# Constant matmuls while the first input is awaited, spread memsets, own weight tiles for the third and fourth product, and systems in four transfers

## The chip, the cores and the metric

The kernel runs on one core of a Trainium2 chip. A core has engines that work side by side, each on its own queue of instructions, in order: TensorE (PE in the profile; PEld is its weight load), VectorE (DVE), ScalarE (ACT), GpSimd (POOL) and SyncE (SP, which here issues all transfers). They wait for each other on semaphores. The metric is the device time of one execution in microseconds (us); lower is better.

## What is computed

One layer of a streaming encoder for a prompt of 2048 frames and 32 sample frames, 1024 wide. The input is normalised and projected once (about 6160 columns); branch A is attention over a band of nine 64-frame chunks, branch B a gated delta rule in chunks of 64; both are gated, merged, projected and normalised again.

```
hp = layer_norm(x_prompt, ln0_g, ln0_b)
qa, ka, va, za, qkv_b, zb, a_b, b_b, gate_a, gate_b = split_projection(x @ w_in)
...
ya = (oa.reshape(bsz, t, A_WIDTH) * jax.nn.silu(za)) @ w_branch_a
...
t_inv = lax.linalg.triangular_solve(eye + m, jnp.broadcast_to(eye, m.shape),
                                    left_side=True, lower=True, unit_diagonal=True)
...
yb = (ob * jax.nn.silu(zb)) @ w_branch_b
mix = jax.nn.sigmoid(gate_a) * ya + jax.nn.sigmoid(gate_b) * yb
y = layer_norm(ALPHA * x + mix @ w_out, ln_g, ln_b)
```

## The kernel before

**Who sets the order.** The program's text does not give the order of the instructions. Each piece of work is a Python generator (a stream) that yields where it must wait: for a gate (a number of buffers), a mark (something is done), a queue, or a time. `Flow.run` takes the stream whose own clock is least, lets it emit instructions up to its next yield, and advances clocks by a price of each instruction (`Engine.price`, lines 225 to 254) and of each transfer (`Flow.transfer`, 203 to 209: 200 KB per us behind the transfers planned before it). So prices decide in which order instructions stand in each engine's queue. On the chip the engines then work through these queues in order, each instruction waiting for its operands. All engine instructions but a few are emitted at line 260, all transfers at line 283; a tile's name therefore tells more than a line.

**The opening.** `build_h(0, ...)` brings the first 1024 frames in as eight tiles `x` of 128 frames. For each: mean and variance on DVE (`BATCH_NORM_STATS2`, `BATCH_NORM_AGGREGATE` into `mv`), a power on POOL, the scaling of `x` on DVE, eight transposes on PE into two PSUM banks (`b` and `a`), scale and shift into `tmp` (the first half by ACT, the second by DVE), the high float16 half `hi` (cast on ACT) and the rest `lo` (POOL). `norm_params` first brings the scale and shift vectors `ln0gT` and `ln0bT` by a transpose of `prm`, and derives their common scale `h_scale` by a small product.

**The projection.** Each column group of 128 of `w_in` is a `Job`. `fetch` loads its weights (`wraw`, two buffers); `divide` finds a power-of-two scale from the sum of squares (ACT `Square` into `whi`, a product `b<-w_sq,tiny` on PE, `w_scale` on DVE, POOL, DVE), scales on ACT, casts to `whi` (ACT) and subtracts into `wlo` (POOL). There are two pairs of `whi` and `wlo`, and `divide` asks for one at `w_gate` before anything else. `multiply` then makes 8 products `whi` x `hi`, 8 `wlo` x `hi` and 8 `whi` x `lo` for each block of columns, into a bank `pj`. The first two jobs are gates of the merge; their blocks, 256, 256 and 512 columns wide, alternate (`two`), so that both use each part of the input as it comes. The third job is `ab` (16 columns: decay and beta of the delta rule, with `whi` alone), the fourth the first of the convolution's. When the last block of a job is multiplied, its pair goes back to `w_gate`. `marked` is the generator that hands the jobs out, two late, so that the last two of a half can be marked.

**Branch B.** When the input of a half is there, `phase_b` opens. `diag` makes 17 tiles that hold block diagonals (`k_bd`, `qk_bd` four each, `q_bd`, `kd_bd`, `u_bd` three each), and clears each with a memset on DVE, one behind the other. Eight blocks of 512 frames (and the sample, in the second half) go through `prep` (decays), `system` (the triangular systems, written to DRAM as `sol_p` in four transfers), `solve` (brings them back so that each of 128 partitions holds one of 32 systems, four times over for four groups of right-hand sides, in `sys_p`; then 31 steps of two DVE instructions on `sys_t` and `sys_u`), `inverse`, and `chain` (the recurrence over chunks, PE and DVE by turns: banks `x`, tiles `r`, `vn`, `state`). Two `solve` streams run side by side. The transfer into `sys_p` has an access pattern whose slowest dimension has four steps of no distance: `[[0, 4], [1024, 32], [1, 1024]]`.

**Then** branch A of the half, the second half with the same two phases, and the merge with the output projection.

The names that the change touches: `Flow.transfer`, `norm_params` (a neighbour is added), `Job`, `divide`, `multiply`, `phase_b` (`diag`, `system`, `solve`, the list of streams that it starts), `marked`, and the opening and the loop at the end of `trunk`.

Of the kernel before, what the change touches and what calls it, by code (L numbers as in the profile page):

```python
# [21 lines left out]
P = 128  # L22
# [34 lines left out]
for _p in range(1, NP):  # L57
    ORDER += [(_p, 0), (_p, 1), (_p, 2), (_p - 1, 3)] + [None] * FILL[_p]
ORDER += [(NP - 1, 3)]
MARGIN = 1.6  # L60
LEAD = 5.0
BLOCKS = [
    [(0, 512, 0), (512, 512, 512)],
# [91 lines left out]
class Flow:  # L155
# [47 lines left out]
    def transfer(self, queue, size):  # L203

        start = max(self.cur.clock + 0.2, self.busy.get(queue, 0.0)) + 0.5
        self.busy[queue] = start
        end = max(start + 0.6, self.busy.get("DMA", 0.0)) + size / 200e3
        self.busy["DMA"] = end
        return end + MARGIN
# [59 lines left out]
def trunk(ctx: ExitStack, tc: tile.TileContext, x_p, x_s, cache_k, cache_v, st_conv, st_gdn,  # L269
# [89 lines left out]
    def power(out, sums):  # L359

        yield bank["b"]
        ps = pt("b")
        PE.matmul(ps[:, 0:1], tiny[:], sums, start=True, stop=True)
        yield
        V.tensor_scalar(out=out, in0=ps[:, 0:1], scalar1=1e-24, scalar2=None, op0=ALU.add)
        bank["b"].give()
        yield
        rsqrt(out, out)
        yield
        V.tensor_scalar(out=out.bitcast(I32), in0=out.bitcast(I32), scalar1=0x7F800000, scalar2=None,  # L370
                        op0=ALU.bitwise_and)

    def norm_params(sp):
# [197 lines left out]
    class Job:  # L571
# [3 lines left out]
        def __init__(self, half, wid, src, evac=None, key=None, cols=P, blocks=None):  # L575
            self.wid = wid
            self.half, self.src, self.evac, self.cols, self.key = half, src, evac, cols, key
            self.end = self.two = False
            self.blocks = blocks or BLOCKS[half]

# [42 lines left out]
    def divide():  # L623

        while True:
            job, raw, t = yield from q_raw.get()
            yield w_gate
            hi = wpool.tile([P, KD, P], F16, tag="whi", bufs=2, name="whi")
            lo = wpool.tile([P, KD, P], F16, tag="wlo", bufs=2, name="wlo")
            sc = w_scale[:, job.wid:job.wid + 1]  # L630
# [36 lines left out]
    def multiply():  # L667

        while True:
            some, todo = [], [(0, 0)]  # L670
            while todo:
# [26 lines left out]
                for k in range(KD):  # L698
                    PE.matmul(ps[:, 0:n], wh[:, k], hl[:, k, :], start=False, stop=(k == KD - 1))
                    if k == KD - 1:  # L700
                        last = bi == len(job.blocks) - 1
                        if job.end and (bi == 0 or last):
                            h_free[0 if bi == 0 else 1].give()
                        if last:
                            w_gate.give()
# [80 lines left out]
    def phase_b(half):  # L786
# [21 lines left out]
        def diag(name, bufs):  # L808
            ts = []
            for i in range(bufs):  # L810
                t = bp.tile([P, 8, P], F32, name=f"{name}{i}")
                V.memset(t[:], 0.0)
                ts.append(t)
            return ts

        k_bd, qk_bd = (diag(n, NPAR) for n in ("k_bd", "qk_bd"))
# [354 lines left out]
        def system(k):  # L1171
# [4 lines left out]
            yield k.qk_ready  # L1176
            yield k.prep
            k.pn = yield from p_slots.take()
            kb, qkb = k.kb, k.qkb = k_bd[k.par], qk_bd[k.par]
# [45 lines left out]
        def solve():  # L1225
            while True:
# [5 lines left out]
                for g in range(4):  # L1232
                    G.memset(sys_u[g * 32:(g + 1) * 32].rearrange("p r i -> p (r i)")[:, g::36], 1.0)
                yield t
                p0 = pd[k.n % (2 * NP)][:]
                yield dma(sys_p[:].rearrange("p j i -> p (j i)"),
                          bass.AP(p0.tensor, p0.offset, [[0, 4], [1024, 32], [1, 1024]]))
                yield from substitute(sys_p, sys_u, sys_t)
# [196 lines left out]

        for g in (worker(todo), worker(decays), prep(), local(), solve(), solve()):
            flow.start(g)
# [506 lines left out]
    def marked():  # L1944

        ahead, half = [], None
        for job in all_jobs():
            if job.half != half:
# [4 lines left out]
                job.two = True  # L1953
            n += 1
            if n <= 2:
                if job.key is None:
# [267 lines left out]


    with ExitStack() as stack0:
        open_banks(stack0, "ps0", a=3)
        xp = stack0.enter_context(tc.tile_pool(name="x0", bufs=1, reuse_waits="tile"))
        flow.start(norm_params(xp))
        flow.start(build_h(0, xp, 8))  # L2230
# [7 lines left out]
    for half in range(2):  # L2238
        stack, make, done = phase_b(half)
        enter(1, half, make)  # L2240
        flow.run(done)
        stack.close()
        if half:
            wr_pool.append(ctx.enter_context(tc.tile_pool(name="wr0", bufs=1)))
# [71 lines left out]
```

## Time and profile before

| what | value |
|---|---|
| time, median of 3 runs | 2083.18 us (2080.98 to 2087.81) |
| the profiled execution | 2081.13 us, of which the span (first to last instruction) is 2079.4 |
| PE busy / idle in the span | 1969.9 / 109.5 us |
| granted TensorE clock, mean over the span | 0.982 |
| DVE, ACT, POOL busy | 1456.5, 977.0, 709.3 us |
| transfers, all queues | 196.5 MB, 95 GB/s on average |

How to read the rows that follow: in the timeline a row has its start in us from the span's start, its length, the engine, line, operation, `out<-in`, the shape, and in brackets how long the engine had been idle before it and what ended that. Matmuls are pipelined, so the length of one is longer than the step from one to the next. In the table of windows a row has the stretch, its length, the busy time of each engine with its number of instructions, the granted clock of TensorE (PEclk), the mean busy share of 16 DMA engines and what they moved in GB/s. In the list of waits a row has who waited for whom, the sum in us, how often, and the longest.

### The profile page before, as it was taken

What the parts mean: (1) busy time and instruction counts of PE and PEld (TensorE: products, weight loads), DVE (VectorE), ACT (ScalarE), POOL (GpSimd) and SP (SyncE); (2) the same over time, 40 slices, a digit from 0 to 9 for tenths busy, and PEclk for the clock granted to TensorE, in tenths of its full rate; (3) what the DMA queues carried; (4) which work ended last, traced back from release to release, by engine and by line L of the source; (5) the groups of instructions that cost most, each with busy time, mean ns of one, the idle gap of its engine ahead of it and who ended that gap; (6) DMA issues with size and microseconds to landing.
All of it is one profiled execution on the core that took longest, in us unless ns stands there. A gap on an engine that the chain in (4) does not pass through costs nothing. (4 is left out here: it accounts for less than half of the span.)

```text
span 2079.4 us, 41810 instructions
## 1 busy us (share of the span) xinstructions
PE 1969.9 (95%) x15098; PEld 1419.4 (68%) x15098; DVE 1456.5 (70%) x4673; ACT 977.0 (47%) x2098; POOL 709.3 (34%) x1075
## 2 busy tenths in 40 slices
PE   4899999999999999899999899999999999999998
PEld 3455666667465666566677676767667678999996
DVE  7579888874267667768998887347657677655565
ACT  5565645444466668564544434346566642111110
POOL 5254443423322123334333323311110224644443
PEclk9899999999999999999999999999999999999999
DMA  3132332232323333222233233332332345433331
GB/s 109 62 98 80 98 107 65 82 82 87 121 68 122 92 87 101 66 72 73 78 85 88 73 91 95 97 91 76 87 89 82 108 139 196 135 105 113 111 123 48
DMA packets 197724, 196.53 MB, mean 95 GB/s; under 512 B 79623, under 2 KB 147571, under 8 KB 197517
## 3 DMA queue, kind: packets, MB, share of 16 engines
q1 hardware_dynamic: 197516, 193.85, 31.7%
q8 instruction: 119, 1.95, 0.4%
q14 instruction: 89, 0.72, 0.1%
HBM read 135.91 MB, written 50.53 MB: 90 GB/s over the span
## 5 line engine op out<-in xcount | busy, mean ns | idle before, releaser
L260 PE MATMUL pj<-hi,whi 128*128 128x512 f16 (+2 forms) x1992 | 654.3, 344 | 12.6 <-POOL whi L260 2.4
L260 PE MATMUL pj<-hi,wlo 128*128 128x512 f16 (+2 forms) x1952 | 644.4, 342 | 2.0 <-POOL wlo L260 1.9
L260 PEld LDWEIGHTS <-whi 128*128 128x128 f16 x3984 | 412.7, 105 | 222.2 <-issue 11.1
L260 PE MATMUL pj<-lo,whi 128*128 128x512 f16 (+2 forms) x1992 | 461.3, 339 | 0.0
L260 POOL TENSOR_TENSOR wlo<-wraw,whi 128x256 f16<-128x256 f32 x384 | 263.8, 708 | 570.9 <-ACT whi L260 328.4
L260 PEld LDWEIGHTS <-wlo 128*128 128x128 f16 x1952 | 207.1, 106 | 112.6 <-issue 11.2
L260 ACT CAST mh<-sg 128x256 fp32r<-128x256 f32 x64 | 26.0, 407 | 273.7 <-DVE sg L260 273.7
L260 ACT ACTIVATE wraw<-wraw,w_scale 128x1024 f32<-128x1024 f32 (+1 forms) x98 | 111.5, 1138 | 64.9 <-DVE w_scale L260 51.9
L260 ACT CAST ph<-b 128x512 f16<-128x512 f32 (+2 forms) x224 | 92.9, 422 | 100.2 <-PE b L260 95.4
L260 PE MATMUL a<-ghi,whi 128*128 128x256 f32 (+1 forms) x512 | 132.5, 290 | 4.9 <-DVE sg L260 4.7
L260 DVE TENSOR_TENSOR pl<-b,ph 128x512 f16<-128x512 f32 (+2 forms) x224 | 107.2, 485 | 37.9 <-ACT ph L260 36.8
L260 PE MATMUL a<-ghi,wlo 128*128 128x256 f32 (+1 forms) x512 | 130.6, 286 | 1.1 <-DVE wlo L260 1.1
L260 ACT CAST whi<-wraw 128x512 f16<-128x512 f32 (+1 forms) x196 | 119.6, 611 | 23.4 <-PE pj L260 20.5
L260 DVE TENSOR_TENSOR sys_u<-sys_u,sys_t 128x60 f32<-128x60 f32 (+24 forms) x527 | 123.3, 240 | 6.1
L260 POOL TENSOR_TENSOR w_scale<-w_scale,mhalf 128x1 f32<-128x1 f32 x49 | 32.4, 662 | 257.0 <-DVE w_scale L260 204.0
L260 ACT ACTIVATE sb<-sb,mx,unit 128x640 f32<-128x640 f32 (+4 forms) x128 | 108.8, 851 | 20.7 <-DVE mx L260 20.3
L260 DVE SCALAR_TENSOR_TENSOR acc<-raw,cwT,acc 128x512 f32<-128x512 f32 x144 | 112.0, 777 | 5.2 <-ACT acc L260 4.1
L260 DVE TENSOR_TENSOR sys_t<-sys_u,sys_p 128x60 f32<-128x60 f32 (+20 forms) x459 | 111.2, 246 | 5.9
L260 PEld LDWEIGHTS a<-ghi,whi 128*128 128x128 f32 x512 | 98.2, 192 | 7.3 <-DVE sg L260 7.0
L260 ACT COPY v_t<-o 128x64 f32<-128x64 f32 x132 | 27.6, 209 | 157.0 <-PE o L260 113.1
L260 PE MATMUL b<-ident,sb 128*128 128x128 f32 x560 | 99.3, 277 | 1.9 <-DVE ga L260 0.9
L260 PEld LDWEIGHTS a<-ghi,wlo 128*128 128x128 f32 x512 | 97.8, 191 | 1.9 <-DVE wlo L260 1.6
(350 smaller groups left out, 4237.0 us busy)
## 6 DMA issues: line engine op xcount, KB each, us to landing
wraw<-in_w_in SPq DMA_DIRECT2D x192, 256.0 KB
sg<-sig SPq DMA_DIRECT2D x112, 128.0 KB
sig<-sig SPq DMA_DIRECT2D x44, 256.0 KB
sys_p<-sol_p SPq DMA_DIRECT2D x17, 512.0 KB
x<-in_x_p SPq DMA_DIRECT2D x16, 512.0 KB
xt<-in_x_p SPq DMA_DIRECT2D x16, 512.0 KB
out_y_p<-xt SPq DMA_DIRECT2D x16, 512.0 KB
glo<-g SPq DMA_DIRECT2D x14, 512.0 KB
```

Source lines behind the costliest of these rows:

```text
L260: r = f(*a, **k)
```

## The change

It has six parts.

1. `warm`: a tile `ones` is set by a memset on DVE, and as long as the first half's input isn't complete, PE multiplies it with itself into a bank `w` wherever the plan has PE idle, one product of 512 columns for each 0.45 us of planned gap (0.25 from 7 us on). 59 products are added.
2. `transfer`: the plan counts 360 KB per us for transfers that start before 25 us, and 200 as before behind that. No instruction is added; the order changes.
3. `zeros`: the 17 memsets are a stream of their own, 1.2 us apart in the plan, and `system` waits for the mark `zeroed`. They are the same instructions.
4. `own`: the third and fourth job of the first half have `whi` and `wlo` tiles of their own (the third only `whi`) and pass `w_gate` by; the third job is handed out without the delay. The order of the jobs is the same.
5. `solve`: the systems come back in four transfers of 32 partitions, 128 KB each, in place of one of 128.
6. The pool of those weight tiles stays open until the first phase of branch B is done.

```diff
+ZERO = 1.2
...
-        end = max(start + 0.6, self.busy.get("DMA", 0.0)) + size / 200e3
+
+        end = max(start + 0.6, self.busy.get("DMA", 0.0)) + size / (360e3 if start < 25.0 else 200e3)
...
+    def warm(sp):
+
+        ones = sp.tile([P, 512], F16, name="ones")
+        V.memset(ones[:], 1.0)
+        ps = pt("w")
+        while l_ready[0][7].at is None:
+            yield flow.cur.clock + 0.45
+            t = flow.cur.clock
+            n = int(max(t - max(flow.busy.get("PE", 0.0), 0.4), 0.0) / (0.45 if t < 7.0 else 0.25))
+            for _ in range(n):
+                nc.tensor.matmul(ps[:], ones[:, 0:P], ones[:], start=True, stop=True)
+            if n:
+                flow.busy["PE"] = t
...
+            self.own = None
...
-            yield w_gate
-            hi = wpool.tile([P, KD, P], F16, tag="whi", bufs=2, name="whi")
-            lo = wpool.tile([P, KD, P], F16, tag="wlo", bufs=2, name="wlo")
+            if job.own:
+                hi, lo = job.own
+            else:
+                yield w_gate
+                hi = wpool.tile([P, KD, P], F16, tag="whi", bufs=2, name="whi")
+                lo = wpool.tile([P, KD, P], F16, tag="wlo", bufs=2, name="wlo")
...
-                        if last:
+                        if last and not job.own:
                             w_gate.give()
...
                 t = bp.tile([P, 8, P], F32, name=f"{name}{i}")
-                V.memset(t[:], 0.0)
                 ts.append(t)
...
+        zeroed = mark()
+
+        def zeros():
+
+            for t in [t for some in (k_bd, qk_bd, q_bd, kd_bd, u_bd) for t in some]:
+                V.memset(t[:], 0.0)
+                yield flow.cur.clock + ZERO
+            zeroed.done()
...
             yield k.prep
+            yield zeroed
...
-                yield dma(sys_p[:].rearrange("p j i -> p (j i)"),
-                          bass.AP(p0.tensor, p0.offset, [[0, 4], [1024, 32], [1, 1024]]))
+
+                for g in range(4):
+                    t = dma(sys_p[g * 32:(g + 1) * 32].rearrange("p j i -> p (j i)"),
+                            bass.AP(p0.tensor, p0.offset, [[1024, 32], [1, 1024]]))
+                yield t
...
-        for g in (worker(todo), worker(decays), prep(), local(), solve(), solve()):
+        for g in (zeros(), worker(todo), worker(decays), prep(), local(), solve(), solve()):
...
+            if half == 0 and 2 < n <= 4:
+                job.own = [first_w.tile([P, KD, P], F16, name=f"{x}{n}") if x == "whi" or job.cols == P else None
+                           for x in ("whi", "wlo")]
+            if half == 0 and n == 3:
+                yield job
+                continue
...
+    stack_w = ExitStack()
+    first_w = stack_w.enter_context(tc.tile_pool(name="first_w", bufs=1, reuse_waits="tile"))
     with ExitStack() as stack0:
-        open_banks(stack0, "ps0", a=3)
+        open_banks(stack0, "ps0", a=3, w=1)
         xp = stack0.enter_context(tc.tile_pool(name="x0", bufs=1, reuse_waits="tile"))
+        flow.start(warm(xp))
...
         stack.close()
+        stack_w.close()
```

**What stands in the queues.** First PE in the opening, from the small product for the common scale to the first projection. `x` with a number is one input tile of 128 frames, `w_sq` the sum of squares of a weight tile. Before:

```order
L260 MATMUL b<-h_scale,tiny 128x1
L260 MATMUL b<-ident,x_154 128x128 x4
L260 MATMUL a<-ident,x_154 128x128 x4
L260 MATMUL b<-ident,x_156 128x128 x4
L260 MATMUL a<-ident,x_156 128x128 x4
L260 MATMUL b<-ident,x_158 128x128 x4
L260 MATMUL a<-ident,x_158 128x128 x4
L260 MATMUL b<-w_sq,tiny 128x1
L260 MATMUL a<-ident,x_160 128x128 x4
L260 MATMUL b<-ident,x_160 128x128 x4
L260 MATMUL b<-ident,x_170 128x128 x4
L260 MATMUL a<-ident,x_170 128x128 x4
```

The first weight's product stood behind the transposes of three input tiles, and the first projection (behind these rows and a transpose of parameters) behind five. After, the same place, from the first tile's transposes:

```order
L262 MATMUL b<-ident,x_160 128x128 x4
L262 MATMUL a<-ident,x_160 128x128 x4
L385 LDWEIGHTS ones
L385 MATMUL w<-ones 128x512
...
L262 MATMUL b<-w_sq,tiny 128x1
L262 MATMUL b<-ident,x_162 128x128 x4
L262 MATMUL a<-ident,x_162 128x128 x4
```

It now stands behind one tile (`x_160` is the first there) and three constants; the first projection stands behind four tiles. Twenty-one of the constants stand ahead of the first tile's transposes (seven of them ahead of the transpose of `prm`), 21 between these and the first projection, 17 between the first blocks.

Second, DVE where the decays of the first half are made, from the evacuation of the `ab` product to the running sum (the row that reads `reset`). Before:

```order
L260 SCALAR_TENSOR_TENSOR ab<-pj,w_inv,ab 40x512
L260 TENSOR_SCALAR ab<-ab,dtb 8x512
L260 TENSOR_SCALAR ab<-ab 8x512
L260 SCALAR_TENSOR_TENSOR row_836<-ab 8x512
L260 SCALAR_TENSOR_TENSOR ab<-pj,w_inv,ab 40x512
L260 TENSOR_SCALAR ab<-ab,dtb 8x512
L260 SCALAR_TENSOR_TENSOR row_837<-ab,row_836 8x512
L260 TENSOR_SCALAR row_837<-row_837,nalog 8x512
L260 SCALAR_TENSOR_TENSOR ab<-reset,row_837 8x512
```

After, the second part of the same stretch:

```order
L262 MEMSET qk_bd_740 128x1024
L262 TENSOR_SCALAR ab<-ab 8x512
L262 SCALAR_TENSOR_TENSOR row_921<-ab 8x512
L262 SCALAR_TENSOR_TENSOR ab<-pj,w_inv,ab 40x512
L262 MEMSET q_bd_741 128x1024
L262 TENSOR_SCALAR ab<-ab,dtb 8x512
L262 SCALAR_TENSOR_TENSOR row_922<-ab,row_921 8x512
L262 TENSOR_SCALAR row_922<-row_922,nalog 8x512
L262 SCALAR_TENSOR_TENSOR ab<-reset,row_922 8x512
```

Three memsets stand in that stretch now (`qk_bd_739`, just ahead of these rows, is the first). On PE the transposes of the decays (`b<-ident,ab`) stood 21 products behind the end of the `ab` job, and stand 44 behind it now; the second ones stood 27 products behind the first, and stand 52 behind them.

Third, SP where the first system comes back (`sol_p` is a block's systems in DRAM). Before:

```order
L283 DMA sol_p_614<-p_c_630 32x8x32 x4
L283 DMA sig_70<-sig 128x512
L283 DMA gcb<-gc_dram 64x512 x2
L283 DMA ext_dram_92<-ext_row 128x768
L283 DMA wraw<-in_w_in 128x512 x2
L283 DMA sig_70<-sig 128x512
L283 DMA sys_p<-sol_p_614 128x1x1024
```

After:

```order
L285 DMA ext_dram_91<-ext_row 128x768
L285 DMA sol_p_750<-p_c_766 32x8x32 x4
L285 DMA wraw<-in_w_in 128x512 x2
L285 DMA gcb<-gc_dram 64x512 x2
L285 DMA sys_p<-sol_p_750 32x1024 x4
```

One transfer has become four, and fewer others stand between the write of the system and its return.

## The prediction

> **What bounds the kernel now.** I read the page's first part, then the table of windows from the start, then the timeline where the windows show an idle TensorE (PE), and last the waits on the system transfers.
>
> ```profile
> PE 1969.9 (95%) x15098; PEld 1419.4 (68%) x15098; DVE 1456.5 (70%) x4673; ACT 977.0 (47%) x2098; POOL 709.3 (34%) x1075
> core 0: us, PE busy (x) PEld busy (x) DVE busy (x) ACT busy (x) POOL busy (x), PEclk, DMA share, GB/s
> 0.00:40.00 40.00, 16.47 (x72) 13.42 (x73) 31.87 (x95) 19.70 (x41) 21.99 (x31) 1.00 0.38 137
> 40.00:80.00 40.00, 32.50 (x173) 19.11 (x172) 22.80 (x44) 16.42 (x34) 13.97 (x19) 0.87 0.19 55
> 80.00:200.00 120.00, 111.80 (x634) 59.13 (x632) 94.94 (x263) 74.91 (x121) 56.36 (x87) 0.94 0.28 83
> ```
>
> PE is the bound: 1970 of 2079 us busy. What can be saved is its 109 us of idle time and the time it runs slowly. The first 80 us hold 31 us of that idle time (23.5 + 7.5), the next 120 us another 8. In the first 40 us DVE is the busiest engine (32 of 40). So the opening is bound by preparing the first inputs on DVE, and everything later by PE: a microsecond that PE gains in the opening is kept unless something behind it makes PE wait again.
>
> ```profile
> 30.00 1.11 PE L260 MATMUL b<-ident,x 128*128 128x128 f32 x4 [6.76 <-DVE x L260]
> 31.90 0.42 PE L260 MATMUL pj<-hi,whi 128*128 128x256 f16 x1
> 32.12 0.42 PE L260 MATMUL pj<-hi,wlo 128*128 128x256 f16 x1
> ...
> 49.72 0.39 PE L260 MATMUL pj<-hi,whi 128*128 128x256 f16 x1 [1.07 <-ACT whi L260]
> ...
> 56.12 0.27 PE L260 MATMUL pj<-hi,wlo 128*128 128x256 f16 x1
> ...
> 57.76 0.27 PE L260 MATMUL pj<-hi,whi 128*128 128x256 f16 x1
> ...
> 60.38 0.38 PE L260 MATMUL pj<-hi,whi 128*128 128x512 f16 x1
> ...
> 69.15 1.89 PE L260 MATMUL pj<-lo,whi 128*128 128x512 f16 x8
> 73.47 3.40 PE L260 MATMUL pj<-hi,whi 128*128 128x512 f16 x8 [2.43 <-POOL whi L260]
> ...
> 82.03 0.38 PE L260 MATMUL pj<-hi,whi 128*128 128x512 f16 x1
> ```
>
> At 31.90 the products of 256 columns step by 0.22 us (31.90 to 32.12); from 57.76 to 60.38 a block of 24 takes 2.62, so 0.109 each. The first products therefore run at half rate, though the window's clock column says 1.00 there: that column shows nothing of a clock that was low from the start. From 49.72 to 56.12 the rate is half again, behind short waits. The first two products (six blocks) end at 71.0 (69.15 + 1.89), having begun at 31.9; at full rate they need 4 x 2.62 + 2 x 5.18 (60.38 to the next block, twice the 2.6) = 21 us.
>
> **The change, part by part.** All terms are against the profiled execution's own 2081.1 us (span 2079.4 and 1.7 around it); the median of the runs is 2.05 above that.
>
> *The opening.* The rows of the other engines that feed these blocks:
>
> ```profile
> 5.28 0.69 DVE L260 BATCH_NORM_STATS2 st<-x 128x6 f32<-128x512 f32 x1 [0.46 <-DMA x<-in_x_p]
> ...
> 17.77 1.05 ACT L260 ACTIVATE whi<-wraw 128x1024 f16<-128x1024 f32 x1
> ...
> 22.50 2.00 DVE L260 TENSOR_SCALAR tmp<-a,ln0gT,ln0bT 128x128 f32<-128x128 f32 x6 [0.38 <-PE a L260]
> ...
> 24.59 1.15 ACT L260 ACTIVATE wraw<-wraw,w_scale 128x1024 f32<-128x1024 f32 x1 [0.45 <-DVE w_scale L260]
> ...
> 46.15 1.37 DVE L260 TENSOR_SCALAR tmp<-a,ln0gT,ln0bT 128x128 f32<-128x128 f32 x4
> 47.68 0.91 DVE L260 MEMSET k_bd<- 128x1024 f32 x1 [0.16 <-issue]
> ...
> 51.59 2.28 POOL L260 TENSOR_TENSOR lo<-tmp,hi 128x512 f16<-128x512 f32 x2
> ```
>
> DVE works from 5.28 to 47.5 (46.15 + 1.37) almost without a gap, and the change gives it the same instructions in another order, plus one memset. Seven constants stand ahead of the parameter transpose, which delays DVE's start by under 1 us, since it waits for the first input anyway. So the last input tile is ready at about 46, by no more than a reordering's 2 us earlier. What changes is what PE does until then. The weight's square moves up on ACT (17.77 now, behind two tiles; then behind the first half tile), its product stands behind one tile's transposes and no longer behind three, and the first block no longer waits for the fifth tile's transposes (30.00). The first tiles still end at about 24.5 (22.50 + 2.00), so the first block starts at 25 or so and not at 31.9, and it and the three other blocks of 256 columns, 10.5 us at full rate, fit ahead of the last tile; now two and a half of them are left when it is ready. The third blocks begin when ACT has cast the last tile, some 3 us behind DVE: at 49, where they begin at 60.38 now. That is **-11** (-7 if DVE ends at 47.5 and part of a block is left over, -13 if everything fits).
>
> The third product waits 2.43 us for its weights at 73.47, and the fourth 0.5:
>
> ```profile
> PE pj L260 <- POOL wlo L260: 0.5, 2, 0.3
> ```
>
> With tiles of their own these weights need not wait for the first two products to end; their loads and divisions lie beside the third blocks, 10 us of PE: **-2.9**.
>
> Then come the decays, whose transposes stand in PE's order:
>
> ```profile
> 89.35 1.26 PE L260 MATMUL b<-ident,ab 40*64 40x40 f32 x32 [1.73 <-DVE ab L260]
> ...
> 92.04 0.63 PE L260 MATMUL pj<-hi,whi 128*128 128x512 f16 x1
> ...
> 93.90 0.38 PE L260 MATMUL pj<-hi,wlo 128*128 128x512 f16 x1
> ...
> 100.72 1.93 PE L260 MATMUL b<-ident,ab 40*64 40x40 f32 x32 [2.56 <-DVE ab L260]
> 102.59 0.61 PE L260 MATMUL pj<-hi,whi 128*128 128x512 f16 x1
> ...
> 107.39 0.38 PE L260 MATMUL pj<-hi,wlo 128*128 128x512 f16 x1
> ```
>
> The waits are 1.73 and 2.56, and a slow stretch follows each. From 92.04 to 93.90 five products take 1.86 where 5 x 0.216 = 1.08 would do (0.8 lost); from 102.59 to 107.39 eleven and a small one take 4.8 where 2.5 would do, and the transposes 1.93 where 1.26 did (3.0 lost). Together 8.1. In the new order 23 and 25 more products stand ahead of these transposes, 5.0 and 5.4 us. Against that, three of the scattered memsets stand in the first chain of DVE and four in the second, 1.07 us each (0.91 and the 0.16 ahead of it). The cover is 5.0 against 1.73 + 3.2, just enough, and 5.4 against 2.56 + 4.3, 1.5 short. I take **-6** (0 to -8.1).
>
> The 17 memsets themselves cost nothing now, since DVE waits behind them, and go to a stretch (57 to 90) where DVE has room; the same block in the second half makes no wait of PE, so spreading it there is worth nothing. At the other end, if DVE has no room, each costs 1.07: up to 18; I take 0, by the 95 of 120 us that DVE is busy from 80 to 200.
>
> How the clock behaves in the new opening no row shows. The constants fill PE's gaps by the written plan, not by what happens; the slow stretch 49.72 to 56.12 costs 3.2 us (half of 6.4). I take one such stretch more, **+3** (0 to +6.4). [...]
>
> Opening: -11 - 2.9 - 6 + 3 = **-17**, between -3.5 (-7 - 2.9 - 0 + 6.4) and -24 (-13 - 2.9 - 8.1).
>
> *Systems in four transfers.*
>
> ```profile
> 424.99 0.56 SPq L283 DMA_DIRECT2D sys_p<-sol_p  x1
> ...
> 437.48 0.24 DVE L260 TENSOR_SCALAR sys_t<-sys_p,sys_u 128x31 f32<-128x31 f32 x1 [4.25 <-DMA sys_p<-sol_p]
> 438.06 0.44 PE L260 MATMUL x<-r,u_bd 128*128 128x64 f32 x2 [3.43 <-DVE r L260]
> ...
> 441.92 0.38 PE L260 MATMUL pj<-hi,wlo 128*128 128x512 f16 x1
> ```
> ```profile
> 436.00:437.40 1.40, 0.00 (x0) 0.00 (x0) 0.00 (x0) 0.00 (x0) 0.00 (x0) 1.00 0.24 91
> ```
> ```profile
> 1183.53 0.56 SPq L283 DMA_DIRECT2D sys_p<-sol_p  x1
> ...
> 1195.00 0.24 DVE L260 TENSOR_SCALAR sys_t<-sys_p,sys_u 128x31 f32<-128x31 f32 x1 [4.83 <-DMA sys_p<-sol_p]
> ...
> 1195.48 0.69 PE L260 MATMUL x<-state,k_bd 128*128 128x64 f32 x2 [4.48 <-DVE state L260]
> ...
> 1199.65 0.28 PE L260 MATMUL pj<-hi,whi 128*128 128x272 f16 x1
> ```
>
> The transfer of 512 KB lands 11 to 12 us behind its issue. While it alone is under way, every engine idle, the 16 DMA engines are 0.24 busy: four work, twelve do not. DVE, which works in order, stands for it 4.25 and 4.83 us, and PE behind DVE 3.43 and 4.48; PE then runs slowly until 441.92 and 1199.65, 3.9 and 4.2 us at half rate. That is 7.9 + 4.0 = 11.9 us. [...]
>
> The price is SP: four issues of 32 partitions took 1.82 us:
>
> ```profile
> 132.82 1.82 SPq L283 DMA_DIRECT2D sol_p<-p_c  x4
> ```
>
> against 0.56, so 1.3 us more for what is queued behind, 17 times; the transfers behind are weights, loaded a product ahead. If the four are spread over all engines, the data lands within the 4 us or so by which DVE came early. But the new order puts other work there, and not every microsecond comes back: I take **-9** (+2 to -11.9).
>
> Sum: -17 - 9 = -26, so 2055 beside the profiled 2081.1, and **2057** as a median, 2 above.
>
> **Rivals.**
>
> *The clock never falls in the opening.* The constants and transposes leave no gap long enough for it, the +3 falls away, and the time is 2054. The slow rows behind 89.35 and 100.72, after waits of 1.73 and 2.56, speak against it; that the gaps of the new opening may be shorter still speaks for it. [...]
>
> *The constants don't do what they say.* They run at half rate, 0.43 each, and 38 of the 59 stand behind the first tile's transposes: 16 us put into PE's gaps. The four blocks of 256 columns then take 5.2 each, 10 us more, and the third blocks begin at 57: -3 in place of -11, and 2065. For it: the rate fell after short waits three times above. Against it: PE is almost never idle in the new opening.
>
> *The opening's gain is given back to DVE.*
>
> ```profile
> 160.00:180.00 20.00, 19.07 (x108) 10.28 (x106) 19.28 (x51) 12.15 (x22) 10.55 (x19) 1.00 0.33 84
> ```
>
> Here DVE is 96% busy; if it is the real bound of this stretch, PE only waits longer, and the transfers' 9 are left: 2074. Against it: PE is 95% busy in the same row.
>
> *Slower: the scattered memsets make DVE late for PE.* Each matmul of the delta rule holds PE's queue until DVE has written its operand. If memsets push DVE behind by more than PE's order allows, PE waits as at 100.72, 2.56 and 3.0 of slow rate behind it, 5.6 us a block; for eight blocks 45, less the 26: 2102. From six such waits on (26 and the 6 that can be told from no change, by 5.6) the kernel is slower than before.
>
> **How the numbers follow.** Forecast 2057 (2048 to 2065) 0.50; no fall of the clock, 2054, 0.14; constants in the way, 2065, 0.13; given back, 2074, 0.09; slower 0.06; the two gains small at once, within 0.3% (6 us, what a measurement of this kernel can tell from no change), 0.08. The range 2042 to 2076 holds all but the last two and the far ends: the opening at -24 and the transfers at -11.9 together would give 2047, and a few us below that are left for waits that the new order happens to remove. Faster 0.86, same 0.08, slower 0.06.
>
> **What would show it.** In the changed profile: the first `pj` product near 25 with a step of 0.11; the third blocks near 49; no POOL `whi` wait ahead of the third product; no `DVE ab` wait above 1 us; the first product behind the decays' (82.03 now) near 66 to 71; no wait of DVE for `sys_p`, and DMA share near 1 while a system comes in. Wrong would be: third blocks later than 55 (DVE's chain or the clock), PE waits for DVE in sum above 15 us between 100 and 500, or the two large waits of PE behind `sys_p` replaced by waits for another operand.

## The result, and the profile after

The changed kernel takes 2056.45 us (median of 4 runs, 2052.2 to 2061.14), the kernel before beside it 2083.44 (4 runs, 2080.98 to 2087.81). The ratio is 0.9864, with a 95% interval of 0.9839 to 0.9889, so 23 to 34 us less. The forecast was 2057. Point by point it was less good than its sum: the opening brought nearly twice what was forecast, and the transfers of the systems nothing.

The first part of the changed kernel's page:

```profile
PE 1977.9 (96%) x15157; PEld 1422.6 (69%) x15157; DVE 1454.2 (71%) x4674; ACT 976.6 (47%) x2098; POOL 711.3 (35%) x1075
```

Its windows from the start:

```profile
core 0: us, PE busy (x) PEld busy (x) DVE busy (x) ACT busy (x) POOL busy (x), PEclk, DMA share, GB/s
0.00:40.00 40.00, 31.77 (x182) 19.28 (x183) 31.94 (x108) 25.37 (x54) 27.56 (x37) 0.96 0.46 155
40.00:80.00 40.00, 39.31 (x238) 20.96 (x237) 24.07 (x55) 26.52 (x45) 18.05 (x29) 1.00 0.20 64
80.00:200.00 120.00, 116.44 (x682) 62.39 (x680) 101.18 (x280) 73.98 (x123) 55.00 (x92) 0.99 0.31 90
```

The span is 2059.3 us, so PE's idle time fell from 109.5 to 81.4 although 59 products were added. From 40 to 80 us PE is now busy 39.3 of 40 (32.5 before) at full clock (0.87 before). PE's timeline of the same kernel answers the rows of the prediction:

```profile
22.30 0.28 PE L262 MATMUL pj<-hi,wlo 128*128 128x256 f16 x1
22.41 0.27 PE L262 MATMUL pj<-hi,whi 128*128 128x256 f16 x1
...
29.73 2.30 PE L385 MATMUL w<-ones 128*128 128x512 f16 x9
...
33.60 1.89 PE L385 MATMUL w<-ones 128*128 128x512 f16 x8
...
45.94 0.38 PE L262 MATMUL pj<-hi,whi 128*128 128x512 f16 x1 [0.69 <-ACT hi L262]
...
54.71 1.89 PE L262 MATMUL pj<-lo,whi 128*128 128x512 f16 x8
56.44 1.89 PE L262 MATMUL pj<-hi,whi 128*128 128x512 f16 x8
...
61.75 1.89 PE L262 MATMUL pj<-lo,whi 128*128 128x512 f16 x8
63.48 0.38 PE L262 MATMUL pj<-hi,whi 128*128 128x512 f16 x1
...
73.07 1.13 PE L262 MATMUL b<-ident,ab 40*64 40x40 f32 x32
...
83.78 1.89 PE L262 MATMUL pj<-lo,whi 128*128 128x512 f16 x8
85.59 1.13 PE L262 MATMUL b<-ident,ab 40*64 40x40 f32 x32
```

The first product runs at full rate from its start at 22 (step 0.11), the third blocks begin at 45.94, the third product at 56.44 and the fourth at 63.48 follow without a wait, and both groups of the decays' transposes stand without one. The last row of the second, the third and the fifth product ends at 56.6, 63.6 and 85.7; before, they ended at 71.0, 82.2 and 115.5. So the fifth product is done **29.8 us sooner**. The second group of the decays' transposes (1.1 us) stood ahead of its end before and stands behind it now, so by equal work it is 28.7 us, and that is already the whole gain.

What the changed order brought in later is in PE's rows too. These waits have no counterpart before:

```profile
205.05 0.66 PE L262 MATMUL x<-r,u_bd 128*128 128x64 f32 x2 [2.29 <-DVE sys_t L262]
...
971.12 0.38 PE L262 MATMUL pj<-hi,whi 128*128 128x512 f16 x1 [2.89 <-ACT sig L262]
...
1076.42 1.07 PE L262 MATMUL b<-tu_t,p_c 32*32 32x32 f32 x32 [2.17 <-DVE tu_t L262]
```

The kernel before has waits of this size at other places, which are gone (2.06 us for `p_c` at 191.26, 2.25 for `kd_bd` at 388.29, 2.28 for `r` at 1018.16, and the two behind `sys_p`). Behind the fifth product PE idles 73.6 us before and 72.5 in the changed kernel: one set of waits was traded for another.

### The profile page after: what moved, and what is told of

Its sections match the earlier page's. It is cut to its first block, busy times and chain, and to the rows that moved or that the text cites. A ratio compares the mean times of both kernels' runs of the same rounds, so it can differ in the third digit from the quotient of the medians.

```text
span 2059.3 us, 42008 instructions
## 1 busy us (share of the span) xinstructions
PE 1977.9 (96%) x15157; PEld 1422.6 (69%) x15157; DVE 1454.2 (71%) x4674; ACT 976.6 (47%) x2098; POOL 711.3 (35%) x1075
## 5 line engine op out<-in xcount | busy, mean ns | idle before, releaser
L262 PEld LDWEIGHTS <-wlo 128*128 128x128 f16 x1952 | 206.3, 106 | 113.6 <-issue 11.2
L262 ACT ACTIVATE wraw<-wraw,w_scale 128x1024 f32<-128x1024 f32 (+1 forms) x98 | 111.6, 1139 | 58.5 <-DVE w_scale L262 54.3
L262 DVE TENSOR_TENSOR sys_u<-sys_u,sys_t 128x60 f32<-128x60 f32 (+23 forms) x527 | 125.5, 242 | 7.8
L262 DVE TENSOR_TENSOR sys_t<-sys_u,sys_p 128x60 f32<-128x60 f32 (+21 forms) x459 | 111.0, 243 | 6.5
L262 DVE CUSTOM_DVE_ANT_0 sb<-a,bias 128x320 f32<-128x320 f32 (+4 forms) x128 | 61.7, 486 | 54.2 <-PE a L262 53.7
```

The costliest lines, as they stand in the source:

```text
L262: r = f(*a, **k)
```

## The experiments

All times stand beside runs of the kernel before on the same chip, and ratios are against those. Four marks in PE's timeline divide each profile: the end of the second product and of the fifth, the first `c<-vt,ph` (branch A of the first half begins) and the first `a<-ghi,whi` (the merge begins). Idle is the span less PE's busy time on the page. The marks are not quite equal work everywhere: in the kernel before, b_sys4_pin, b_price, b_m17, a_noown and a_block the second group of the decays' transposes (1.1 us) stands ahead of the fifth product's end, in the others behind it, and in a_m17 and b_m17 the merge mark stands 85 and 116 products earlier in PE's order. The plan also sets the number of constants: it is 59, but 77 in a_price200 and 57 in a_m17.

| kernel | median us | ratio, 95% interval | 2nd ends | 5th ends | branch A | merge | span | idle |
|---|---|---|---|---|---|---|---|---|
| before | 2083.44 | 1 | 71.0 | 115.5 | 581.4 | 1677.4 | 2079.4 | 109.5 |
| changed | 2056.45 | 0.9864, 0.9839 to 0.9889 | 56.6 | 85.7 | 556.6 | 1655.6 | 2059.3 | 81.4 |
| a_again | 2054.83 | 0.9853, 0.9832 to 0.9873 | 56.6 | 85.7 | 552.4 | 1647.3 | 2049.8 | 79.8 |
| b_sys4_pin | 2073.42 | 0.9933, 0.9914 to 0.9953 | 70.9 | 111.6 | 578.1 | 1667.5 | 2070.8 | 99.1 |
| a_sys1_pin | 2057.14 | 0.9856, 0.9836 to 0.9877 | 56.6 | 85.7 | 555.9 | 1651.7 | 2055.3 | 80.4 |
| a_nowarm_pin | 2055.64 | 0.9852, 0.9833 to 0.9871 | 59.2 | 88.3 | 556.5 | 1651.8 | 2053.9 | 89.6 |
| a_min | 2060.25 | 0.9885, 0.9859 to 0.9912 | 59.2 | 88.3 | 559.9 | 1658.1 | 2060.2 | 88.2 |
| a_price200 | 2068.99 | 0.9930, 0.9909 to 0.9951 | 68.4 | 97.5 | 571.4 | 1666.2 | 2068.2 | 85.5 |
| a_noown | 2072.82 | 0.9949, 0.9931 to 0.9967 | 56.7 | 101.6 | 572.5 | 1669.2 | 2070.6 | 87.9 |
| a_block | 2054.29 | 0.9855, 0.9831 to 0.9879 | 56.8 | 100.9 | 559.9 | 1648.1 | 2052.6 | 86.0 |
| b_price | 2096.76 | 1.0056, 1.0029 to 1.0083 | 58.2 | 108.5 | 598.9 | 1697.6 | 2099.9 | 115.9 |
| a_half | 2050.71 | 0.9846, 0.9819 to 0.9874 | 58.0 | 87.0 | 555.4 | 1647.5 | 2050.0 | 77.5 |
| a_m17 | 2061.21 | 0.9895, 0.9872 to 0.9918 | 58.3 | 87.4 | 551.1 | 1651.0 | 2062.3 | 87.2 |
| b_m17 | 2093.56 | 1.0050, 1.0030 to 1.0070 | 69.2 | 110.0 | 586.7 | 1672.2 | 2090.6 | 113.8 |

**The same kernel again (a_again).** No edit.

> The changed kernel once more, for a second profile of the same order and a time on the same chip. If the slow stretches of the clock fall on a grid of the chip's own (3.4 us), they come in part at other places than in the first profile while PE's waits are the same to 0.3 us each, and time and profile differ by several us between executions. If they are set by the waits alone, each stands behind the same wait as before. Time 2056, within 4 us.

The marks of the opening are the same to 0.1 us and PE's idle time is 1.6 us less, yet the span is 9.5 us shorter. The rest, 7.9 us, is in PE's busy time (1977.9 against 1970.0 for the same instructions), so it is the clock: by the trace's record of the granted clock, PE ran at half rate for 69.9 us of the first profile and 54.0 of the second, and half of the difference is 8.0. It can be seen behind one wait. PE's timeline in the first profile of the changed kernel:

```profile
169.33 1.30 PE L262 MATMUL b<-sel,v_t 128*64 128x2 f32 x16 [1.47 <-ACT v_t L262]
...
170.97 0.63 PE L262 MATMUL pj<-hi,whi 128*128 128x512 f16 x1
171.40 0.63 PE L262 MATMUL pj<-hi,wlo 128*128 128x512 f16 x1
```

Three windows of the same profile, the second behind that wait (PEclk is the third number from the end):

```profile
26.70:30.10 3.40, 3.40 (x16) 2.37 (x17) 3.17 (x17) 0.13 (x1) 3.40 (x5) 0.50 0.00 0
170.00:173.40 3.40, 3.40 (x15) 1.59 (x14) 2.24 (x13) 0.00 (x0) 1.74 (x2) 0.51 0.66 190
204.20:211.00 6.80, 5.95 (x24) 4.68 (x25) 4.31 (x17) 1.18 (x4) 0.19 (x1) 0.50 0.67 187
```

The second profile, its timeline at the same wait:

```profile
169.35 1.09 PE L262 MATMUL b<-sel,v_t 128*64 128x2 f32 x16 [1.47 <-ACT v_t L262]
...
170.82 0.38 PE L262 MATMUL pj<-hi,wlo 128*128 128x512 f16 x1
171.04 0.38 PE L262 MATMUL pj<-hi,whi 128*128 128x512 f16 x1
```

And its window:

```profile
170.00:173.40 3.40, 3.40 (x24) 2.02 (x24) 2.26 (x13) 0.00 (x0) 1.73 (x2) 1.00 0.68 193
```

The wait is 1.47 us in both. Once the products behind it step by 0.43 us and 15 matmuls fit into 3.4 us, once by 0.22 and 24 do. So the expectation held that the slow stretches are not set by the waits alone, and a comparison of two single profiles carries several us of chance. Idle time carries little of it (1.6 us here), the later marks most of it (8.3 us at the merge).

**Four transfers in the order of before (b_sys4_pin), and one transfer in the changed order (a_sys1_pin).**

```diff
-yield dma(sys_p[:]..., bass.AP(..., [[0, 4], [1024, 32], [1, 1024]]))
+for g in range(4):
+    nc.sync.dma_start(sys_p[g * 32:(g + 1) * 32]..., bass.AP(..., [[1024, 32], [1, 1024]]))
+yield flow.transfer("SP", 4 * P * 1024)
```

> The kernel before with the systems brought back in four transfers of 32 partitions, but planned as one, so that every engine's instructions stand in the order of before and only the 17 transfers differ. Theory T (the transfers have the worth that the prediction gave them, and the changed kernel lost it again through its other order): the waits of DVE for sys_p (4.25 and 4.83 us) and of PE behind it (3.43 and 4.48) are gone, so are the slow stretches behind them, and nothing takes their place: 2072 us, 9 to 12 below before. Theory H (the transfers were hidden anyway; PE meets the next operand that is late): within 3 us of before, with new waits of PE of 2 us or more right behind the places of the old ones.

```diff
-for g in range(4):
-    t = dma(sys_p[g * 32:(g + 1) * 32]..., bass.AP(..., [[1024, 32], [1, 1024]]))
+nc.sync.dma_start(sys_p[:]..., bass.AP(..., [[0, 4], [1024, 32], [1, 1024]]))
+for g in range(4):
+    t = flow.transfer("SP", P * 1024)
 yield t
```

> The changed kernel with the systems in one transfer again, planned as four, so that only these transfers differ. In the changed kernel DVE reaches the first step of a system 9.2 to 17.4 us behind the issue; at a landing of 11.5 us, as before, DVE would wait in 11 of 17 systems, 10 us in all and 2.3 at most. Theory T: PE sees about half of it and a slow stretch or two: 5 to 12 us slower than the changed kernel, 2061 to 2068. Theory H: within 3 us of it, 2053 to 2060.

In the order of before the four transfers are worth 12.4 us (2085.77 to 2073.42), as theory T said. In that kernel, SP's row of the four issues at the place where DVE waited 4.25 us before:

```profile
424.64 1.78 SPq L1237 DMA_DIRECT2D sys_p<-sol_p  x4
```

The window behind it, while the system comes in, with a DMA share of 0.83:

```profile
424.60:428.60 4.00, 4.00 (x73) 2.63 (x72) 3.87 (x11) 2.35 (x7) 1.76 (x2) 1.00 0.83 200
```

And DVE's first step on that system, in its timeline:

```profile
432.81 0.43 DVE L260 TENSOR_SCALAR sys_t<-sys_p,sys_u 128x31 f32<-128x31 f32 x1
```

DVE starts the system 8.2 us behind the issue without a wait, where it started 12.5 us behind it after a wait of 4.25. PE's idle time falls by 10.4 us, 3.4 of it between the fifth product and branch A and 6.7 between branch A and the merge, where the two waits stood. (The fifth product ends 3.9 us sooner in this profile, ahead of any system's transfer. That much is not the transfers' doing.)

In the changed order the same edit is worth nothing that can be told: with one transfer the kernel takes 2057.14 beside 2054.83, and PE idles 0.6 us more. DVE waits for `sys_p` six times, and this row of its timeline is the longest wait:

```profile
1075.11 0.45 DVE L262 TENSOR_SCALAR sys_t<-sys_p,sys_u 128x31 f32<-128x31 f32 x1 [1.28 <-DMA sys_p<-sol_p]
```

DVE comes to the systems 9 to 17 us behind the issue, and where it waits here, the one transfer has landed 10.3 to 10.6 us behind it. The two big waits of before were waits of its order, not of the transfer alone. So theory H held here, and T there.

**No constants (a_nowarm_pin), and neither constants nor four transfers (a_min).**

```diff
-for _ in range(n):
+for _ in range(n if t < 0.9 else 0):
     nc.tensor.matmul(ps[:], ones[:, 0:P], ones[:], start=True, stop=True)
```

(The plan has no gap of that length ahead of 0.9 us, so no product is emitted.)

> The changed kernel without the 59 constant products, every other instruction in the same order. Theory S (the constants only fill slack; the opening's gain is the order and the weights): PE runs slowly from 22 to about 32, which costs 5 us, but between 22 and 46 it has some 9 us of room (4.0 of constants, 3.2 of waits, 1.7 of a slow stretch), so the third blocks still begin at 46 to 48: 0 to 3 us slower, 2056 to 2059. Theory C (the full clock is what brings the gain): the whole 8 us of slow clock that the opening had before come back: 2064. Theory W (the constants stand in the way): 2 to 4 us faster, 2053.

> The changed kernel without the constant products and with one transfer for the systems, every other instruction in the same order: what is left of the change is the order, the own weight tiles and the place of the memsets. Theory K (these three are the whole gain): fifth product at 88, DVE's and PE's waits for a system small, time 2058, between 2054 and 2062. Rival (constants and transfers are needed together, since one covers for the other): 2066 or more.

PE's timeline without the constants:

```profile
36.61 0.42 PE L262 MATMUL pj<-hi,whi 128*128 128x256 f16 x1
36.82 0.42 PE L262 MATMUL pj<-hi,wlo 128*128 128x256 f16 x1
...
37.21 0.27 PE L262 MATMUL pj<-hi,wlo 128*128 128x256 f16 x1
37.32 0.27 PE L262 MATMUL pj<-hi,whi 128*128 128x256 f16 x1
...
48.59 0.38 PE L262 MATMUL pj<-hi,whi 128*128 128x512 f16 x1 [0.69 <-ACT hi L262]
```

The step is 0.21 us, half rate, until 37 us and 0.11 from there. The third blocks begin 2.6 us later than with constants (45.94), and the fifth product ends 2.6 us later. The time is 2055.64 against 2054.83: the 2.6 us are less than it can show. Theory S holds, though the third blocks begin 0.6 us beyond its 48; C is out by the time, W by the marks. Without the four transfers as well it is 2060.25: theory K, within its bounds. Order, weight tiles and the place of the memsets are some four fifths of the change (1.15% of 1.36 to 1.47); whether the rest is real, the overlapping intervals leave open.

**The parts of the order, one undone at a time (a_price200, a_noown, a_block), and the price alone (b_price).**

```diff
-size / (360e3 if start < 25.0 else 200e3)
+size / 200e3
```

> The changed kernel with the old price of the first transfers (200 KB per us everywhere); everything else of the change is in. In the profiles the first two products end at 71.0 before and 56.6 in the changed kernel, the third at 82.2 and 63.6, the fifth (behind the decays' transposes) at 115.5 and 85.7. Theory O (the order that this price makes brings the first 14 us): the first two products end at 66 or later and the fifth at 95 or later, and the time is 2064 to 2068. Theory N (constants, weight tiles and memsets bring it, the price little): first two products by 59, fifth by 89, time 2055 to 2059.

```diff
-if half == 0 and 2 < n <= 4:
-    job.own = [first_w.tile(...) ...]
-if half == 0 and n == 3:
-    yield job
-    continue
```

> The changed kernel with the third and fourth product in the common pair of weight tiles, and the third handed out two jobs late as before. Theory O: the first two products end at 56.6 as before this edit, the third waits for its weights again, 4 us (18.6 between the third product's ends is 14.4 from the first two and 4.2 from here): third at 67 to 68, fifth at 90; time 2059. Rival: the later order hides it, third at 67 but fifth at 86 to 87 and the time 2055.

```diff
 for t in [...]:
     V.memset(t[:], 0.0)
-    yield flow.cur.clock + ZERO
+yield
 zeroed.done()
```

> The changed kernel with the 17 memsets of each half in one block again. Theory O (the waits at the decays' transposes, 1.73 and 2.56 us with 5 us of slow clock, went because more products stand ahead of them, not through the memsets): fifth product at 85 to 88, time 2053 to 2057. Rival M (the memsets were in the way of the decays): the waits of 1.5 to 2.6 us are back, fifth product at 92 to 96, time 2062 to 2066.

```diff
-size / 200e3
+size / (360e3 if start < 25.0 else 200e3)
```

> The kernel before with the new price of the first transfers alone. Theory O: the first two products end 8 to 12 us sooner than 71.0, at 59 to 63, and the kernel takes 2072 to 2076 by it. Theory N: at 68 or later, 2081 to 2086.

*The price* makes the first gain: without it the second product ends at 68.4 (11.8 later, with 18 more constants in the gaps) and the kernel takes some 16 us more by the ratios (0.9930 against 0.9853). Given to the kernel before it brings the second product from 71.0 to 58.2, 12.8 us with no constants at all. But there the third product then stands for its weights, since both pairs of tiles are in use, and the kernel is slower in the end. PE's row there:

```profile
66.17 3.60 PE L260 MATMUL pj<-hi,whi 128*128 128x512 f16 x8 [8.00 <-POOL whi L260]
```

Theory O was right on the first two products and wrong on the time (2072 to 2076 expected, 2096.76 measured): from the end of the fifth product to branch A this order takes 490.4 us (598.9 - 108.5) where before's takes 465.9. The two windows, before and b_price:

```profile
115.50:581.40 465.90, 447.56 (x3116) 284.38 (x3114) 338.82 (x1257) 231.76 (x456) 182.97 (x296) 0.98 0.33 93
108.50:598.90 490.40, 461.57 (x3116) 291.18 (x3114) 340.98 (x1257) 231.77 (x456) 177.65 (x296) 0.95 0.31 88
```

PE idles 10.5 us more there, and the same 3116 matmuls keep it busy 14.0 us longer, at a lower clock (0.95 against 0.98).

*The own tiles* were expected to cost 4 us if undone. Undone, the kernel takes some 20 us more by the ratios (0.9949 against 0.9853). The third product ends only 1.0 us later (64.6), but in the order that the plan then makes, the second group of the decays' transposes comes to PE long before its operand is there. The row in the timeline of a_noown:

```profile
86.91 1.94 PE L262 MATMUL b<-ident,ab 40*64 40x40 f32 x32 [8.14 <-DVE ab L262]
```

On DVE the last steps towards that operand stood for ACT, by this row:

```profile
84.32 0.68 DVE L262 SCALAR_TENSOR_TENSOR row<-ab,row 8x512 f32<-8x512 f32 x1 [1.58 <-ACT row L262]
```

The window that the wait falls into, at half clock to its end:

```profile
83.00:93.20 10.20, 6.29 (x43) 3.47 (x44) 6.87 (x13) 6.78 (x11) 2.26 (x3) 0.50 0.23 73
```

*The memsets* in one block delay the fifth product by 15.2 us (14.1 by equal work), by these two waits in PE's timeline of a_block and the slow clock behind the first (a granted clock of 0.50 from 68.0 to 81.7 us):

```profile
67.61 0.39 PE L262 MATMUL pj<-hi,whi 128*128 128x512 f16 x1 [3.90 <-ACT whi L262]
...
74.08 1.94 PE L262 MATMUL b<-ident,ab 40*64 40x40 f32 x32 [6.08 <-DVE ab L262]
```

So rival M was right that the memsets are in the way, though the delay is larger than its 92 to 96, and theory O was right on the time: a_block takes 2054.29, no more than the changed kernel. At the beginning of branch A 7.5 us of the delay are left (559.9 against 552.4 of a_again), at the merge 0.8 (1648.1 against 1647.3).

**The second half in the order of before (a_half).**

```diff
 V.memset(t[:], 0.0)
-yield flow.cur.clock + ZERO
+if not half:
+    yield flow.cur.clock + ZERO
```

> The changed kernel with the memsets spread in the first half and in one block in the second, which puts the second half's instructions, from the sample's decays on, back into the order of before. There the profiles show 13.7 to 13.9 us of idle PE with four transfers (before's order) and 15.6 in the changed order, and no wait of 2.9 for sig or 2.2 for tu_t. Expected 2 to 5 us faster than the changed kernel, 2050 to 2053; if the clock's grid decides, no difference, 2055.

It takes 2050.71, the lowest median of all, but its ratio, 0.9846 (0.9819 to 0.9874), isn't apart from theirs: a faster kernel is not shown. The waits of 2.89 for `sig` and 2.17 for `tu_t` are gone, and in PE's timeline the one for `r` is back that the kernel before had at 1018.16:

```profile
993.25 0.41 PE L262 MATMUL x<-r,u_bd 128*128 128x64 f32 x2 [2.28 <-DVE r L262]
```

PE idles 77.5 us (79.8 and 81.4 in the two profiles of the changed kernel), but between branch A and the merge, where the edit acts, it is 33.8 against 34.0 of a_again. PE's order is the same up to there, and yet the second product ends 1.4 us later. That is the clock, by the same window in a_half and in a_again:

```profile
12.10:18.90 6.80, 6.13 (x22) 3.72 (x21) 5.92 (x18) 5.36 (x13) 4.22 (x6) 0.50 0.70 267
12.10:18.90 6.80, 4.78 (x30) 3.03 (x29) 6.59 (x21) 6.47 (x16) 4.22 (x5) 1.00 0.72 278
```

**The order alone (a_m17, b_m17).**

```diff
-MARGIN = 1.6
+MARGIN = 1.7
```

> The changed kernel with the plan's allowance for a transfer at 1.7 us in place of 1.6: nothing but the order differs, from the first loads on. Theory L (an order is a draw: waits of 1 to 8 us come and go with it): the opening stays (fifth product at 84 to 92), the time moves by 5 us or more either way, somewhere in 2045 to 2075. Rival (the order behind the opening hardly matters): 2052 to 2058.

> The kernel before with the plan's allowance at 1.7 us: only the order differs. Theory L: 2083 plus or minus 5 to 15 us. Rival: 2080 to 2086.

Both are slower than their twins, by 9 us of the ratio (0.9895 against 0.9853, with intervals that just touch) and by 10 us (1.0050). In the changed kernel the opening stays (fifth product at 87.4), branch A even begins sooner than ever (551.1), and then the second half and the merge lose it: from branch A to the end it takes 1511.2 us against 1497.4 in a_again. One of the waits there, from PE's timeline of a_m17:

```profile
1240.29 1.40 PE L262 MATMUL b<-tu_t,p_c 32*32 32x32 f32 x32 [3.21 <-DVE sys_u L262]
```

Theory L held: a plan that differs by a tenth of a microsecond gives another order, and the time moves by some 10 us.

## Why the prediction came out right

**What bounds the kernel** was read rightly: the opening, by DVE's preparing of the inputs, then PE. The third blocks still wait for the last cast tile (45.94, `ACT hi`).

**The third blocks, forecast -11, measured -14.4.** The mechanism was right, a size was off: DVE's last input tile was forecast for 46 and is done at 42.8, by the last row of its kind in DVE's timeline of the changed kernel:

```profile
42.04 0.72 DVE L262 TENSOR_SCALAR tmp<-a,ln0gT,ln0bT 128x128 f32<-128x128 f32 x2
```

The sentence "by no more than a reordering's 2 us earlier" was the slip: it came 4.7 us earlier. It took the same instructions to need the same time, and DVE to have almost no gap. But DVE idled 6.2 of those 42.2 us (busy 36.05 from 5.28 to 47.52), and the eight scalings of `x` alone take 3.9 us less now. DVE's groups from 5.28 to 47.52, before and changed:

```profile
L260 DVE TENSOR_SCALAR x<-x,mv 128x1024 f32<-128x1024 f32 x8 | 10.4, 1294 | 0.4 <-POOL mv L260 0.4
L262 DVE TENSOR_SCALAR x<-x,mv 128x1024 f32<-128x1024 f32 x8 | 6.5, 828 | 0.1
```

The means go with the price: 1.24 to 1.32 us in before, b_sys4_pin, b_m17 and a_price200, 0.83 to 0.87 in the runs with the new price, b_price among them. What makes them longer in the old order is not shown. That the price's order makes the gain is shown (a_price200, b_price); of the 14.4 the constants hold 2.6.

**The third product's weights, forecast -2.9, measured -4.2** in place (from the second product's end to the third's: 11.2 before, 7.0 now). The step did not see that the tiles also decide where the decays' transposes stand: without them 14.8 us of equal work are lost at the fifth product.

**The decays, forecast -6, measured -11.2, or -10.1 by equal work** (from the third product's end to the fifth's, 33.3 before and 22.1 now, where the second group no longer stands in it). The window of before over this stretch:

```profile
82.20:115.50 33.30, 28.48 (x165) 13.74 (x165) 22.14 (x45) 22.75 (x33) 16.25 (x25) 0.85 0.18 53
```

And that of the changed kernel:

```profile
63.60:85.70 22.10, 22.10 (x135) 10.45 (x132) 17.90 (x35) 17.37 (x24) 7.15 (x14) 1.00 0.09 26
```

PE's 4.8 us of idle time are gone, and so are 5.0 us of slow clock (0.15 of 33.3). The forecast priced both at 8.1, with 3.8 us for the slow clock where 5.0 were lost, and took 6, because it held the cover of the second group 1.5 us short; it was enough.

**The clock, forecast +3:** one slow stretch came, from 26.7 to 30.1, at 0.50. PE had room behind it (the constants alone filled 4.2 us between 29.73 and 35.5), so it cost little at the third blocks; that it cost nothing is not shown, as the two more stretches of a_half (0.50 from 12.1 to 18.9) left 1.4 us.

**The memsets, forecast 0:** right for the time, not for the reason. In a block they are in the way of the decays by 14 us, because PE now comes there sooner; the later order makes it up.

**The transfers, forecast -9: this step failed.** The waits of 4.25 and 4.83 were priced as a property of the transfer. Taken alone they are worth 12.4, but the new order does not wait there even with the old transfer, so in this change they are worth about nothing. The prediction had said that "the new order puts other work there", and drew the wrong end from it. One of its signs of being wrong fired in part: waits for `sys_t`, `sig` and `tu_t` of 2.2 to 2.9 us stand in the new order. The others did not: PE's waits for DVE between 100 and 500 are 8.7 us in sum. The signs of being right held: no wait of DVE for `sys_p`, no `DVE ab` above 1 us ahead of the first half's decays, the fourth product at 63.48 (sooner than the 66 to 71), and a DMA share near 1 while a system comes in, in a window of the changed kernel behind the issue of a system. Weights are under way in it too; the second row is of b_sys4_pin, where the four transfers are alone:

```profile
419.00:421.00 2.00, 2.00 (x16) 1.57 (x14) 1.95 (x11) 1.04 (x4) 1.45 (x1) 1.00 1.00 266
252.40:254.40 2.00, 2.00 (x17) 1.57 (x17) 1.41 (x9) 1.94 (x4) 0.35 (x1) 1.00 0.98 248
```

That the four transfers spread over all engines was only an "if" in the forecast. The second row shows it: with the four alone, 16 engines have a mean share of 0.98, against 0.24 while the one transfer of before was alone.

**"A microsecond that PE gains in the opening is kept"** held for this order by the second profile: 28.7 us of equal work at the fifth product, 29.0 at branch A, 30.1 at the merge, 29.6 at the end. The first profile ends 9.5 us later, 7.9 by the clock and 1.6 by waits. It is no rule: a_block was 14 us late at the fifth product and lost nothing by it, and b_price was 7 us ahead of before there and 20 behind it at the end. So where the sum has -17 for the opening and -9 for the transfers, the runs show -29 and about 0. What bounds the kernel was right, but that the sum came so near, 2057 against 2056.45, is luck: two errors of opposite sign, 12 too little and 9 too much, stood in it.

**The rivals.** The clock fell, so the first is out. Constants in the way: not seen; the first seven ran at half rate (3.17 us from 1.62), but of those behind the first tile's transposes seven took 1.67 us from 19.93, which is full rate. The gain given back in the stretch from 160 to 200: not seen. Slower through late memsets: not in this kernel. A late DVE with slow clock behind it is real (waits of 8.14 for `ab` in a_noown and 6.08 in a_block, a granted clock of 0.50 behind both), but only in a_block is it the memsets' doing.

What stays open is why the plan's later orders differ by so much. From the fifth product to branch A they take 459.0 (a_block) to 490.4 us (b_price). The windows above show where the time goes (waits, and slow clock: 0.95 in b_price against 0.98 in before), but no part of the change accounts for it.

## What to carry to other kernels

Where a planner sets the order, price a wait as a property of the order it stands in: undo the part in the new order and add it in the old one, with all other instructions held in place, before giving it a number. Keep marks of equal work (the end of the n-th product) along the profile, since a gain early and a loss later are otherwise one small number. And expect a plan's slightest change to draw a new order, which cost some 10 us in both tries here.

## What the runs showed of the hardware

In the traces' records of the granted clock the slow stretches, at 0.50, are 3.41, 6.83 or 10.24 us long, but for the last of each profile, which the end of the record cuts. In these profiles they lie on a grid: the windows above begin at 26.7, 170.0 and 204.2, 143.3 and 34.2 apart, which is 42 and 10 times 3.413, and all 14 slow stretches in the changed kernel's first profile, and all 15 in that of the kernel before, begin whole multiples of 3.413 us (to 0.04) behind the first of their profile. PE waited 1.47 us ahead of the second of these windows (0.51 from 170.0 to 173.4); in another execution the clock behind the same wait was 1.00. In both, PE was busy 1.94 of the 3.41 us of the grid's step that held the wait, so what decided is not in these rows. Executions of one kernel on one chip spread over 9.3 us (a_again, 2051.54 to 2060.86), about what the clock alone made between its two profiles (7.9).
